# An experts' loop in a pinned order, its output product from two exact parts, and three overflow blocks inside it

## The chip, the core and the metric

The kernel runs on one core of a Trainium2 chip. The metric is the device time of one execution in microseconds (us). Instructions are issued to five engines: PE (matrix products), DVE and ACT (elementwise work), POOL (GpSimd: elementwise work and indirect DMAs) and SP (which only starts DMAs here).

## What is computed

A trunk of two layers over 1024 tokens of width 1024, in f32. Each layer has a modulated norm, one projection that feeds differential attention and an RWKV-7 state scan, an output projection, and then a mixture of 32 experts, of which each token uses two. The part that matters:

```python
def routed_experts(ht, gate_w, expert_id, w_gate, w_up, w_down):
    # each token goes to 2 of 32 experts; rows are sorted by expert, in blocks of ROW_BLOCK = 128
    # per block of one expert:
    #   h = silu(x @ w_gate) * (x @ w_up)      x: 128 x 1024,  h: 128 x 256
    #   y = (h @ w_down) * gate weight         y: 128 x 1024
    ...
```

The reference's sum over the two experts of a token is added to the residual.

## The kernel before

Each layer ends with the experts' loop, `moe` (L1583). It is written for 32 experts with 128 slots each. Tokens of an expert beyond 128 go to overflow blocks, which are run behind the loop, as many as the routing asks for: with these inputs three a layer, so that 35 blocks are computed (70 scatters L1659 in the two layers).

One round of the loop, for expert e:

- `gather` (L1595): POOL fetches 128 rows of the normed input by an indirect DMA into `xg`, two buffers.
- `prepare` (L1603 to L1612): PE transposes them in eight 128x128 pieces (`xT`); ACT makes `xT_hi`, the part that fp32r holds exactly, and DVE the rest, `xT_lo`.
- `split_half` (L1580, L1581): the gate and up weights of an expert come as two halves of 128x2048 (`w_gu`, 1 MB each). Of each, ACT makes `w_hi` and DVE makes `w_lo` = `w_gu` - `w_hi`. There are three pairs of `w_hi` and `w_lo`, so the half that is split during `up(e)` needs the one that `up(e)` has just read.
- `up` (L1628 to L1630): 24 fp32r matmuls of 128x512: `xT_hi` x `w_hi`, `xT_lo` x `w_hi`, `xT_hi` x `w_lo`, in eight slices each.
- `hidden` (L1618 to L1620): ACT's tanh and two DVE instructions give `th`, 128x256.
- `down` (L1649 to L1659), for expert e-1: PE transposes `th` (`hT_ps`), DVE copies it (L1651), PE multiplies it with `w_d` (L1655, `y_ps`) in full f32: four matmuls, eight passes in the trace. DVE scales the result into `yo` (L1658), of which there is one, and POOL scatters its rows to `yd` in DRAM by an indirect DMA (L1659).

The raw weights lie in five `w_gu` and three `w_d` buffers; SP starts their loads four and two experts ahead. An overflow block (L1705 on) computes `up` in full f32 from the raw halves (L1642, 16 passes), under an `If` on the number of blocks.

The order of the instructions on each engine is made by the scheduler of the Tile framework from the order of the code and its dependencies; inside `moe` nothing else sets it.

In the profile's rows, PEld is the weight load of PE, and `w_gu`, `w_hi`, `w_lo`, `w_d`, `xT`, `th`, `yo`, `yd` are the tiles named above. L323, L1210 and L1476 are helpers of earlier stages: splits of other weights on POOL, and one-hot rows of the routing on DVE. L90 is a step of a square root on DVE, L1290 adds a product in PSUM (`po`) to the residual.

Of the kernel before, what the change touches and what calls it, by code (L numbers as in the profile page):

```python
# [10 lines left out]
F32 = mybir.dt.float32  # L11
F32R = mybir.dt.float32r
# [3 lines left out]
OP = mybir.AluOpType  # L16
# [36 lines left out]
class Trunk:  # L53
# [1436 lines left out]
    def route_overflow(self, w, psum):  # L1490
# [20 lines left out]
        big = [w.tile([128, 1024], F32, name="ro_big", tag="ro") for _ in range(2)]  # L1511
        in1, in2 = (x[0:1, 0:480].rearrange("p (b e) -> p b e", e=32) for x in big)
# [9 lines left out]
        tmp = big[0][:, 512:1024].rearrange("p (t e) -> p t e", e=32)  # L1522
# [44 lines left out]
    def load_gu(self, l, i, e):  # L1567

        for half in range(2):
            self.nc.sync.dma_start(self.raw[(2 * i + half) % 5], self.expert_source(l, e, "moe_w_gu")[half])  # L1570

    def load_d(self, l, i, e):
        self.nc.sync.dma_start(self.wd[i % 3], self.expert_source(l, e, "moe_w_down"))

    def split_half(self, n, eng=None):

        nc = self.nc
        raw = self.raw[n % 5]
        lo, hi = self.parts[n % 3]
        nc.scalar.copy(hi, raw)  # L1580
        (eng or nc.vector).tensor_tensor(lo, raw, hi.bitcast(F32), op=OP.subtract)  # L1581

    def moe(self, l, side, psum):  # L1583

        nc, tc = self.nc, self.tc
        with ExitStack() as s:
# [28 lines left out]
            def hidden(ph):  # L1615
                x = tx.tile([128, 512], F32, name="th", tag="mt")
                th = x[:, 0:256]
# [3 lines left out]
                return x  # L1621

            def up(e, x):
                hi, lo = x
                ph = psum.tile([128, 512], F32, name="h_ps", tag="h", bufs=2)
                for k in range(NK):
                    wlo, whi = self.parts[(2 * e + k // 4) % 3]
# [3 lines left out]
                return hidden(ph)  # L1631

            def prepare_late(e):
                pt = transposed(e)
                nc.scalar.copy(late[e % 2], pt)
                return late[e % 2]

            def up_late(e, x):

                ph = psum.tile([128, 512], F32, name="h_ps", tag="h", bufs=2)  # L1640
                for k in range(NK):
                    nc.tensor.matmul(ph, x[:, k, :], self.raw[(2 * e + k // 4) % 5][:, k % 4, :], start=(k == 0), stop=(k == NK - 1))  # L1642
                return hidden(ph)

            def down(e, th):
                w = self.wd[e % 3]
# [10 lines left out]
                yo = tx.tile([128, D], F32, name="yo", tag="x", bufs=1)  # L1657
                nc.vector.scalar_tensor_tensor(yo, po, self.wsl[:, e:e + 1], gt2, op0=OP.mult, op1=OP.mult)  # L1658
                st = nc.gpsimd.indirect_dma_start(out=self.yd, out_offset=bass.IndirectOffsetOnAxis(ap=self.idx_s[:, e:e + 1], axis=0),  # L1659
                                                  in_=yo, in_offset=None, bounds_check=2 * T - 1, oob_is_err=False)  # L1660
                for o in scat:
                    tc.declare_no_dep(st.ins, o.ins, reason="every slot holds another row")
                scat.append(st)
# [4 lines left out]
            def overflow(b):  # L1668
                eb = block_weights(b)
                self.load_gu(l, 32 + b, eb)  # L1670
                self.load_d(l, 32 + b, eb)

            gather(0)
            gather(1)
            x, prev = prepare(0), None
            for e in range(32):
                th = up(e, x)
                for n in (2 * e + 3, 2 * e + 4):
                    if n < 64:
# [20 lines left out]
            gather(33)  # L1700
            self.load_d(l, 32, block_weights(0))
            down(*prev)
            x = prepare_late(32)

            n = nc.values_load(self.ovf[0:1, 0:1], min_val=0, max_val=15)  # L1705
            with ExitStack() as ifs:
                for b in range(15):
                    ifs.enter_context(tc.If(n > b))
                    if b + 2 < 15:
                        gather(34 + b)  # L1710
                    if b + 1 < 15:
                        overflow(b + 1)
                    down(32 + b, up_late(32 + b, x))
                    if b + 1 < 15:
                        x = prepare_late(33 + b)
# [38 lines left out]
    def layer(self, l, x_src):  # L1754

        nc = self.nc
# [12 lines left out]
        def more():  # L1769

            self.wo_stack.close()
            self.more_tiles(se.enter_context(self.pool(name=f"wE{l}", bufs=1, side=here)))
            self.load_gu(l, 1, 1)
            for n in range(3):
                self.split_half(n, nc.gpsimd)
            for e in (2, 3):
                self.load_gu(l, e, e)

        with ExitStack() as s:
            psum = Banks(**{n: s.enter_context(self.pool(name=f"ps{n}e{l}", bufs=b, space=PSUM))  # L1780
                            for n, b in (("tp", 2), ("po", 4), ("pl", 2))})
            self.out_proj(l, there, psum, lambda: (self.load_gu(l, 0, 0), self.load_d(l, 0, 0)), more)
        if l == 0:
            self.dump("xm", self.xm)
        with ExitStack() as s:
            psum = s.enter_context(self.pool(name=f"psE{l}", bufs=1, space=PSUM))
            wp = s.enter_context(self.pool(name=f"wD{l}", bufs=1, side=here))
            self.wd += [wp.tile([128, 2, D], F32, name=f"w_d{i}") for i in range(1, 3)]
            for e in (1, 2):
                self.load_d(l, e, e)  # L1790
            self.moe(l, there, psum)
# [114 lines left out]
```

## Time and profile before

| | us |
|---|---|
| median of three runs | 2879.71 (2871.75 to 2885.03) |
| the profiled execution | 2890.55, span 2888.7 |
| experts' stage, layer 0: first `h_ps` to end of last `y_ps` | 1034.2 to 1441.9 |
| experts' stage, layer 1 | 2427.1 to 2831.3 |

Of the span PE is busy for 85%, DVE 64%, ACT 37%, POOL 25%; the granted clock is 0.903 of full speed on average. The costliest lines are those of the experts' loop and of the input projection. The loop is the stretch where the DMA engines are busiest, between 0.85 and 0.99 of the time.

How to read it: a row of a timeline gives start, duration, engine, line, operation, tiles and shape, and in brackets how long the engine sat idle ahead of it and what ended that. The durations of PE's matmuls overlap; their distance is what counts. In the loop the same pattern returns every 11.07 us.

### The profile page before, as it was taken

The page shows a single profiled execution, that of the slowest core. Times are in us where ns is not written, and L with a number is a line of the kernel's source. Part 1 is how long each engine was busy: PE and PEld are TensorE (multiplying, and loading weights), DVE is VectorE, ACT ScalarE, POOL GpSimd, SP SyncE. Part 2 cuts the span into 40 slices and gives each one's busy share as a digit, 9 for nine tenths or more (in the row PEclk, how much of TensorE's full clock was granted, in tenths as well). Part 3 has the DMA queues.
Part 4 walks back from the last instruction along what each step waited for, and adds up shares of the span by engine and source line. Part 5 has one row for each costly group of instructions (what it writes and reads, how often), then busy time and mean ns, then how long its engine had stood idle before and what let it go on. Part 6 is the DMA issues. An engine that isn't in the chain of part 4 may idle for free.

```text
span 2888.7 us, 45371 instructions
## 1 busy us (share of the span) xinstructions
PE 2452.3 (85%) x17281; PEld 1842.3 (64%) x17281; DVE 1845.5 (64%) x3927; ACT 1063.5 (37%) x1908; POOL 721.3 (25%) x569
## 2 busy tenths in 40 slices
PE   5999987998789779999849888889877986999991
PEld 3766666787678656666427666778756775666650
DVE  5358785555684767767264689756467566776745
ACT  3333332343463224444133343334345331444421
POOL 4122232222420511111141222221242032111113
PEclk8989998998899779999969989899889986999996
DMA  8477575452442359899551434453443224998874
GB/s 285 157 233 215 178 239 135 134 147 93 161 127 93 140 190 328 312 329 336 188 203 52 136 122 140 151 155 115 127 158 114 98 100 147 342 350 317 306 261 186
DMA packets 264230, 548.99 MB, mean 190 GB/s; under 512 B 77048, under 2 KB 181440, under 8 KB 233280
## 3 DMA queue, kind: packets, MB, share of 16 engines
q1 hardware_dynamic: 235424, 490.90, 50.6%
q0 software_dynamic: 23952, 40.99, 3.9%
q10 hardware_dynamic: 4624, 14.06, 1.2%
q8 instruction: 141, 2.31, 0.3%
q14 instruction: 89, 0.73, 0.1%
HBM read 467.68 MB, written 120.09 MB: 203 GB/s over the span
## 4 chain that ended last, share of the span: by engine, by line
PE 52%; DVE 23%; DMA 11%; ACT 7%; issue 5%; POOL 1%; SPq 1%; DVEq 0%; ACTq 0%; POOLq 0%
PE y_ps L1655 8%; PE pj L335 5%; PE pj L336 5%; PE pj L337 5%; DVE w_lo L1581 4%; ACT w_hi L1580 4%; PE h_ps L1629 3%; PE h_ps L1628 2%; DVE sv_m L724 2%; DVE sv_t L726 2%; PE h_ps L1630 2%; PE po L1284 2%; DMA ada_w<-in_ada_w 2%; DMA yd<-yo,idx_s 2%; PE po L1285 2%
## 5 line engine op out<-in xcount | busy, mean ns | idle before, releaser
L1581 DVE TENSOR_TENSOR w_lo<-w_gu,w_hi 128x2048 fp32r<-128x2048 f32 x122 | 279.6, 2292 | 206.3 <-ACT w_hi L1580 202.1
L1580 ACT CAST w_hi<-w_gu 128x2048 fp32r<-128x2048 f32 x128 | 244.0, 1908 | 384.6 <-PE h_ps L1629 367.4
L335 PE MATMUL pj<-hh,wa_hi 128*128 128x512 f32 x800 | 341.6, 427 | 2.7 <-ACT wa_hi L322 1.9
L336 PE MATMUL pj<-hl,wa_hi 128*128 128x512 f32 x800 | 332.0, 415 | 1.1 <-DVE hl L312 1.1
L337 PE MATMUL pj<-hh,wa_lo 128*128 128x512 f32 x800 | 328.9, 413 | 3.3 <-POOL wa_lo L323 3.3
L1655 PE MATMUL y_ps<-w_d,th 128*128 128x512 f32 x560 | 260.3, 608 | 40.9 <-DVE th L1651 25.5
L1628 PE MATMUL h_ps<-w_hi,xT_hi 128*128 128x512 f32 x512 | 225.8, 441 | 3.9 <-ACT xT_hi L1611 3.9
L1629 PE MATMUL h_ps<-w_hi,xT_lo 128*128 128x512 f32 x512 | 210.8, 412 | 2.6 <-DVE xT_lo L1612 2.6
L1630 PE MATMUL h_ps<-w_lo,xT_hi 128*128 128x512 f32 x512 | 203.2, 397 | 0.0
L1655 PEld LDWEIGHTS y_ps<-w_d,th 128*128 128x128 f32 x560 | 101.3, 190 | 156.9 <-issue 103.3
L323 POOL TENSOR_TENSOR wa_lo<-wa_raw,wa_hi 128x1024 fp32r<-128x1024 f32 x50 | 122.0, 2441 | 315.6 <-ACT wa_hi L322 262.0
L335 PEld LDWEIGHTS pj<-hh,wa_hi 128*128 128x128 f32 x800 | 157.8, 197 | 42.0 <-issue 7.4
L337 PEld LDWEIGHTS pj<-hh,wa_lo 128*128 128x128 f32 x800 | 156.8, 196 | 39.5 <-POOL wa_lo L323 4.6
L336 PEld LDWEIGHTS pj<-hl,wa_hi 128*128 128x128 f32 x800 | 157.8, 197 | 37.2 <-issue 4.5
L1659 POOL DMA_INDIRECT yd<-yo,idx_s x70 | 70.5, 1008 | 402.2 <-DVE yo L1658 323.6
L1595 POOL DMA_INDIRECT xg<-h2d,idx_g x74 | 80.1, 1082 | 299.2 <-PE hT_ps L1649 250.7
L1629 PEld LDWEIGHTS h_ps<-w_hi,xT_lo 128*128 128x128 f32 x512 | 98.2, 192 | 50.5 <-DVE xT_lo L1612 30.9
L1658 DVE SCALAR_TENSOR_TENSOR yo<-y_ps,wsl,gt 128x1024 f32<-128x1024 f32 x70 | 89.5, 1279 | 52.2 <-PE y_ps L1655 27.0
L1628 PEld LDWEIGHTS h_ps<-w_hi,xT_hi 128*128 128x128 f32 x512 | 98.4, 192 | 36.7 <-issue 12.9
L724 DVE TENSOR_TENSOR sv_m<-sv_t,sv_n 64x31 f32<-64x31 f32 (+15 forms) x248 | 104.5, 421 | 23.0 <-DMA sv_n<-sp_z 18.5
L1154 ACT ACTIVATE at_p<-at_s,at_mx 128x256 f32<-128x256 f32 (+7 forms) x128 | 94.9, 742 | 63.7 <-DVE at_mx L1152 63.2
L1152 DVE TENSOR_REDUCE at_mx<-at_s 128x1 f32<-128x256 f32 (+7 forms) x128 | 95.8, 753 | 31.3 <-PE at_s L1150 30.4
(438 smaller groups left out, 5428.7 us busy)
## 6 DMA issues: line engine op xcount, KB each, us to landing
w_gu<-in_moe_w_gu SPq DMA_DIRECT2D x144, 1024.0 KB
w_d<-in_moe_w_down SPq DMA_DIRECT2D x72, 1024.0 KB
ada_w<-in_ada_w SPq DMA_DIRECT2D x80, 512.0 KB
wa_raw<-in_w_in SPq DMA_DIRECT2D x50, 512.0 KB
sp_z<-z SPq DMA_DIRECT2D x32, 768.0 KB
b_zz<-sp_z SPq DMA_DIRECT2D x32, 512.0 KB
cy<-yd SPq DMA_DIRECT2D x16, 1024.0 KB
qkv<-qst SPq DMA_DIRECT2D x48, 256.0 KB
```

The costliest lines, as they stand in the source:

```text
L323: nc.gpsimd.tensor_tensor(lo, raw, hi.bitcast(F32), op=OP.subtract)
L335: nc.tensor.matmul(ps, hi[:, k, :], self.hh[k][:, sl], start=(k == 0), stop=False)
L336: nc.tensor.matmul(ps, hi[:, k, :], self.hl[k][:, sl], start=False, stop=False)
L337: nc.tensor.matmul(ps, lo[:, k, :], self.hh[k][:, sl], start=False, stop=(k == NK - 1))
L724: eng.tensor_tensor(t3, tt[:, 0:j + 1, j].unsqueeze(2).to_broadcast([64, j + 1, 31 - j]), nt[:, j, j + 1:32].unsqueeze(1).to_broadcast([64 ...
L1152: nc.vector.tensor_reduce(mx, ps[:, 0:n], axis=AX.X, op=OP.max, negate=True)
L1580: nc.scalar.copy(hi, raw)
L1581: (eng or nc.vector).tensor_tensor(lo, raw, hi.bitcast(F32), op=OP.subtract)
L1628: nc.tensor.matmul(ph, hi[:, k, :], whi[:, k % 4, :], start=(k == 0), stop=False)
L1629: nc.tensor.matmul(ph, lo[:, k, :], whi[:, k % 4, :], start=False, stop=False)
L1630: nc.tensor.matmul(ph, hi[:, k, :], wlo[:, k % 4, :], start=False, stop=(k == NK - 1))
L1655: nc.tensor.matmul(po[:, 512 * half:512 * half + 512], hT[:, k, :], w[:, k, 512 * half:512 * half + 512], start=(k == 0), stop=(k == 1))
```

## The change

Four things change, all in `moe` and what it calls.

1. The output product is made like `up`: `split_d` makes `w_dh` (ACT, L1603) and `w_dl` = `w_d` - `w_dh` (POOL, L1605); `turned` makes the two parts of `hT` (ACT L1679, DVE L1680); PE then runs 12 fp32r matmuls (L1703) `hi` x `w_dh`, `lo` x `w_dh`, `hi` x `w_dl` for four f32 ones. There are two `w_dh` and one `w_dl`; `w_gu` falls from five buffers to four, `w_d` from three to two.
2. The loop runs N = 35 rounds: the three overflow blocks are rounds of it, with weights loaded by the expert's number that SP reads from `ovf`. What is left of the late path starts at the fourth block.
3. Gathers are issued three experts ahead (two before).
4. `in_order` ties the instructions of PE, ACT, DVE and POOL inside the loop to the order in which the code is written, which is new too.

```diff
+    @contextmanager
+    def in_order(self, last):
+        engines = [e.engine for e in (self.nc.tensor, self.nc.scalar, self.nc.vector, self.nc.gpsimd)]
+        traced = self.nc.cur_bb.bb.instructions
+        n = len(traced)
+        yield
+        for i in traced[n:]:
+            if i.engine in engines:
+                if i.engine in last:
+                    self.tc.add_manual_dep(i, last[i.engine].name, ...)
+                last[i.engine] = i
...
+    RAW = 4
...
+    def split_d(self, i, part):
+        hi = self.wdh[i % 2]
+        if part == 0:
+            self.nc.scalar.copy(hi, self.wd[i % 2])
+        else:
+            self.nc.gpsimd.tensor_tensor(self.wdl, self.wd[i % 2], hi.bitcast(F32), op=OP.subtract)
...
+            def turned(e):
+                pt = hidden_turned(e)
+                nc.scalar.copy(hT[:, 0], pt)
+                nc.vector.tensor_tensor(hT[:, 1], pt, hT[:, 0].bitcast(F32), op=OP.subtract)
...
+            def down(e):
+                whi, wlo = self.wdh[e % 2], self.wdl
+                po = psum.tile([128, D], F32, name="y_ps", tag="y", bufs=1)
+                hi, lo = hT[:, 0], hT[:, 1]
+                for n, (x, w) in enumerate(((hi, whi), (lo, whi), (hi, wlo))):
+                    for half in range(2):
+                        cs = slice(512 * half, 512 * half + 512)
+                        for k in range(2):
+                            nc.tensor.matmul(po[:, cs], x[:, k, :], w[:, k, cs], start=(n + k == 0), stop=(n + k == 3))
+                scaled(e, po)
...
-            for e in range(32):
-                th = up(e, x)
-                for n in (2 * e + 3, 2 * e + 4):
-                    if n < 64:
-                        self.split_half(n)
-                if e + 1 < 32:
-                    if e + 2 < 32:
-                        gather(e + 2)
-                    x = prepare(e + 1)
...
-                if prev is not None:
-                    down(*prev)
+            for e in range(N):
+                with self.in_order(last):
+                    ph = up(e, x)
+                    if e + 1 < N:
+                        self.split_half(2 * e + 3)
+                    if e:
+                        turned(e - 1)
+                    if e + 1 < N:
+                        x = prepare(e + 1)
+                    if e + 3 < N:
+                        gather(e + 3)
+                    hidden(e, ph)
+                    self.split_d(e, 0)
...
+                with self.in_order(last):
+                    if e:
+                        down(e - 1)
+                    self.split_d(e, 1)
+                    if e:
+                        scatter(e - 1)
+                    if e + 2 < N:
+                        self.split_half(2 * e + 4)
+                for n in (2 * e + 7, 2 * e + 8):
+                    if n < 2 * N:
+                        self.load_gu(l, n, expert(n // 2))
+                if e + 2 < N:
+                    self.load_d(l, e + 2, expert(e + 2))
```

DVE, one round in the middle of the loop of layer 0, in the program before (`th` of L1651 is the copy of `hT`):

```order
L1658 SCALAR_TENSOR_TENSOR yo<-y_ps,wsl,gt_10476 128x1024
L1581 TENSOR_TENSOR w_lo_10322<-w_gu_10329,w_hi_10323 128x2048
L1651 COPY th<-hT_ps 128x256
L1581 TENSOR_TENSOR w_lo_10326<-w_gu_10330,w_hi_10327 128x2048
L1619 SCALAR_TENSOR_TENSOR th<-th,h_ps 128x256
L1612 TENSOR_TENSOR xT_lo<-xT_ps,xT_hi 128x1024
L1620 TENSOR_TENSOR th<-th,h_ps 128x256
```

and in the program after (L1595 is `w_lo`, L1686 `yo`, L1680 the second part of `hT`, L1638 `xT_lo`):

```order
L1686 SCALAR_TENSOR_TENSOR yo<-y_ps,wsl,gt_10475 128x1024
L1595 TENSOR_TENSOR w_lo_10325<-w_gu_10328,w_hi_10324 128x2048
L1595 TENSOR_TENSOR w_lo_10327<-w_gu_10329,w_hi_10326 128x2048
L1680 TENSOR_TENSOR hT<-hT_ps,hT 128x256
L1638 TENSOR_TENSOR xT_lo<-xT_ps,xT_hi 128x1024
L1644 SCALAR_TENSOR_TENSOR th<-th,h_ps 128x256
L1645 TENSOR_TENSOR th<-th,h_ps 128x256
```

The step that makes `hT` has moved from between the two `w_lo` to behind both.

PE, from the end of one `up` to the start of the next, before:

```order
L1629 MATMUL h_ps<-w_hi_10327,xT_lo 128x512
L1630 MATMUL h_ps<-w_lo_10326,xT_hi 128x512
L1603 MATMUL xT_ps<-ident,xg_10478 128x128 x8
L1649 MATMUL hT_ps<-ident,th 128x128 x2
L1655 MATMUL y_ps<-w_d_9797,th 128x512 x4
L1628 MATMUL h_ps<-w_hi_10325,xT_hi 128x512
```

and after:

```order
L1655 MATMUL h_ps<-w_lo_10323,xT_hi 128x512
L1673 MATMUL hT_ps<-ident,th 128x128 x2
L1629 MATMUL xT_ps<-ident,xg_10477 128x128 x8
L1703 MATMUL y_ps<-w_dh_10470,hT 128x512 x8
L1703 MATMUL y_ps<-w_dl,hT 128x512 x4
L1653 MATMUL h_ps<-w_hi_10324,xT_hi 128x512
```

The transposes of `hT` now stand ahead of those of `xT`, and the output product has become 12 matmuls, of which the last four read `w_dl`.

POOL, in the same stretch after; before, only the scatter L1659 and the gather L1595 stood here, in turn:

```order
L1621 DMA xg_10476<-h2d_614,idx_g 128x1024
L1605 TENSOR_TENSOR w_dl<-w_d_10467,w_dh_10470 128x2048
L1689 DMA yd_615<-yo,idx_s 2048x1024
L1621 DMA xg_10477<-h2d_614,idx_g 128x1024
L1605 TENSOR_TENSOR w_dl<-w_d_9797,w_dh_10469 128x2048
```

The split of `w_d` stands ahead of each scatter.

## Rows read from the trace of the kernel before

**Rows 1.** Chain that ended last, a period of the loop: start us, us, what.

```profile
1186.64 0.23 PE h_ps L1628
...
1187.13 1.92 ACT w_hi L1580
...
1189.08 2.13 DVE w_lo L1581
...
1191.29 0.43 DVE th L1651
```

**Rows 2.** Windows, one period: length, busy us of PE, PEld, DVE, ACT, POOL, PEclk, DMA, GB/s.

```profile
1191.77:1202.84 11.07, 10.45 (x43) 7.02 (x43) 7.91 (x7) 5.00 (x5) 2.08 (x3) 1.00 0.85 311
```

**Rows 3.** Timeline of PE, ends of the stage: start us, us, instruction [idle before].

```profile
1034.22 0.79 PE L1628 MATMUL h_ps<-w_hi,xT_hi 128*128 128x512 f32 x1
...
1061.88 0.48 PE L1628 MATMUL h_ps<-w_hi,xT_hi 128*128 128x512 f32 x1
...
1428.78 7.03 PE L1642 MATMUL h_ps<-w_gu,xT 128*128 128x512 f32 x16
...
1438.21 3.70 PE L1655 MATMUL y_ps<-w_d,th 128*128 128x512 f32 x8 [0.52 <-DVE th L1651]
...
2427.10 0.80 PE L1628 MATMUL h_ps<-w_hi,xT_hi 128*128 128x512 f32 x1
...
2827.61 3.70 PE L1655 MATMUL y_ps<-w_d,th 128*128 128x512 f32 x8 [0.52 <-DVE th L1651]
```

**Rows 4.** Timelines of DVE and POOL at two places where both work.

```profile
983.48 13.87 DVE L1476 TENSOR_SCALAR r_ohr<-r_io,r_rk 128x128 f32<-128x128 f32 x6
...
983.25 13.43 POOL L1581 TENSOR_TENSOR w_lo<-w_gu,w_hi 128x2048 fp32r<-128x2048 f32 x3 [8.43 <-ACT w_hi L1580]
...
850.63 0.68 DVE L1290 TENSOR_TENSOR xm<-xm,po 128x512 f32<-128x512 f32 x1
851.23 1.76 DVE L90 TENSOR_TENSOR rs_u_sub<-rs_u_sub,rs_y_sub 128x4 f32<-128x4 f32 x1
...
853.42 0.16 DVE L90 TENSOR_TENSOR rs_u_sub<-rs_u_sub,rs_y_sub 128x4 f32<-128x4 f32 x1
...
850.55 2.42 POOL L1210 TENSOR_TENSOR wo_0at_q<-wo_raw,wo_0at_q 128x1024 fp32r<-128x1024 f32 x1 [16.62 <-ACT wo_0at_q L1209]
```

**Rows 5.** Scatters and the `yo` that waited; last, groups of 1070 to 1380.

```profile
1352.28 1.01 POOL L1659 DMA_INDIRECT yd<-yo,idx_s  x1 [5.09 <-DVE yo L1658]
...
1362.08 1.28 DVE L1658 SCALAR_TENSOR_TENSOR yo<-y_ps,wsl,gt 128x1024 f32<-128x1024 f32 x1 [0.21 <-DMA yd<-yo,idx_s]
...
1385.75 1.01 POOL L1659 DMA_INDIRECT yd<-yo,idx_s  x1 [5.35 <-DVE yo L1658]
...
1395.94 1.28 DVE L1658 SCALAR_TENSOR_TENSOR yo<-y_ps,wsl,gt 128x1024 f32<-128x1024 f32 x1 [5.09 <-DMA yd<-yo,idx_s]
...
L1658 DVE SCALAR_TENSOR_TENSOR yo<-y_ps,wsl,gt 128x1024 f32<-128x1024 f32 x28 | 35.8, 1279 | 0.2 <-DMA yd<-yo,idx_s 0.2
```

**Rows 6.** DMA queues, 1100 to 1380: packets, MB, share of 16 engines.

```profile
q1 hardware_dynamic: 10660, 77.60, 76.9%
q0 software_dynamic: 7349, 12.02, 11.6%
```

**Rows 7.** Line of the `ovf` reads on SP: ns least, median, most.

```profile
L1666 SPq TENSOR_LOAD <-ovf x10: 265/274/651, 1029.6 to 2796.9; - x10
```

**Rows 8.** Timeline of PE behind two waits of some 2 us.

```profile
313.02 1.09 PE L668 MATMUL tp<-ident,bkb 128*128 128x128 f32 x4 [2.03 <-DVE z L661]
...
315.61 0.63 PE L336 MATMUL pj<-hl,wa_hi 128*128 128x512 f32 x1
...
859.39 0.50 PE L1147 MATMUL at_s<-at_k,at_q 128*128 128x512 f32 x1 [1.92 <-ACT at_p L1154]
859.73 0.39 PE L1150 MATMUL at_s<-at_l,at_q 128*128 128x512 f32 x1
```

More of the change, by code (lines that the diff above doesn't have):

```diff
@@ L2 @@
 import math
-from contextlib import ExitStack, nullcontext
+from contextlib import ExitStack, contextmanager, nullcontext
 import numpy as np
@@ L1565, in expert_source, with load_gu, split @@
         return w if isinstance(e, int) else w[0]
-    def load_gu(self, l, i, e):
-        for half in range(2):
-            self.nc.sync.dma_start(self.raw[(2 * i + half) % 5], self.expert_source(l, e, "moe_w_gu")[half])
+    def load_gu(self, l, n, e):
+        self.nc.sync.dma_start(self.raw[n % self.RAW], self.expert_source(l, e, "moe_w_gu")[n % 2])
     def load_d(self, l, i, e):
-        self.nc.sync.dma_start(self.wd[i % 3], self.expert_source(l, e, "moe_w_down"))
-    def split_half(self, n, eng=None):
[L1577 to L1581, printed above, removed]
+        self.nc.sync.dma_start(self.wd[i % 2], self.expert_source(l, e, "moe_w_down"))
+    def split(self, raw, parts, eng):
+        hi, lo = parts
+        self.nc.scalar.copy(hi, raw)
+        eng.tensor_tensor(lo, raw, hi.bitcast(F32), op=OP.subtract)
+    def split_half(self, n, eng=None):
+        self.split(self.raw[n % self.RAW], self.parts[n % 3], eng or self.nc.vector)
+    def split_d(self, i, part):
[4 more added lines that the diff above has]
+            self.nc.gpsimd.tensor_tensor(self.wdl, self.wd[i % 2], hi.bitcast(F32), op=OP.subtract)
     def moe(self, l, side, psum):
@@ L1630, in up @@
                     nc.tensor.matmul(ph, hi[:, k, :], wlo[:, k % 4, :], start=False, stop=(k == NK - 1))
[L1631 removed]
+                return ph
             def prepare_late(e):
                 pt = transposed(e)
[L1635 to L1636 removed]
+                nc.scalar.copy(late, pt)
+                return late
             def up_late(e, x):
@@ L1641, in up_late, with hidden_turned @@
                 for k in range(NK):
[L1642 to L1646, printed above, removed]
+                    nc.tensor.matmul(ph, x[:, k, :], self.raw[(2 * e + k // 4) % self.RAW][:, k % 4, :], start=(k == 0), stop=(k == NK - 1))
+                hidden(e, ph)
+            def hidden_turned(e):
                 pt = psum.tile([128, 2, 128], F32, name="hT_ps", tag="hT", bufs=1)
@@ new lines, in moe, with scaled, scatter @@
+            yos = {}
+            def scaled(e, po):
+                yo = yos[e] = tx.tile([128, D], F32, name="yo", tag="x", bufs=1)
+                nc.vector.scalar_tensor_tensor(yo, po, self.wsl[:, e:e + 1], gt2, op0=OP.mult, op1=OP.mult)
+            def scatter(e):
+                st = nc.gpsimd.indirect_dma_start(out=self.yd, out_offset=bass.IndirectOffsetOnAxis(ap=self.idx_s[:, e:e + 1], axis=0),
+                                                  in_=yos.pop(e), in_offset=None, bounds_check=2 * T - 1, oob_is_err=False)
+                for o in scat:
+                    tc.declare_no_dep(st.ins, o.ins, reason="every slot holds another row")
+                scat.append(st)
@@ L1656, in down @@
                                          start=(k == 0), stop=(k == 1))
[L1657 to L1663, printed above, removed]
+                scaled(e, po)
+                scatter(e)
             def block_weights(b):
@@ L1669, in overflow, with expert @@
                 eb = block_weights(b)
-                self.load_gu(l, 32 + b, eb)
+                for half in range(2):
+                    self.load_gu(l, 64 + 2 * b + half, eb)
                 self.load_d(l, 32 + b, eb)
+            N = 32 + self.MORE_E
+            def expert(e):
+                return e if e < 32 else block_weights(e - 32)
             gather(0)
             gather(1)
-            x, prev = prepare(0), None
-            for e in range(32):
-                th = up(e, x)
-                for n in (2 * e + 3, 2 * e + 4):
-                    if n < 64:
-                        self.split_half(n)
-                if e + 1 < 32:
-                    if e + 2 < 32:
-                        gather(e + 2)
-                    x = prepare(e + 1)
+            x, last = prepare(0), {}
@@ L1700, in moe @@
[L1700 to L1703, printed above, removed]
+            turned(N - 1)
+            down(N - 1)
+            scatter(N - 1)
+            late = self.lay.tile([128, 8, 128], F32, name="xT", tag="sg")
             n = nc.values_load(self.ovf[0:1, 0:1], min_val=0, max_val=15)
             with ExitStack() as ifs:
-                for b in range(15):
+                for b in range(self.MORE_E, 15):
                     ifs.enter_context(tc.If(n > b))
-                    if b + 2 < 15:
-                        gather(34 + b)
+                    if b == self.MORE_E:
+                        gather(32 + b)
+                        overflow(b)
+                    x = prepare_late(32 + b)
@@ L1772, in more @@
             self.more_tiles(se.enter_context(self.pool(name=f"wE{l}", bufs=1, side=here)))
-            self.load_gu(l, 1, 1)
+            for n in range(2, 4):
+                self.load_gu(l, n, n // 2)
             for n in range(3):
                 self.split_half(n, nc.gpsimd)
-            for e in (2, 3):
-                self.load_gu(l, e, e)
+            for n in range(4, 7):
+                self.load_gu(l, n, n // 2)
         with ExitStack() as s:
@@ L1787, in layer @@
             wp = s.enter_context(self.pool(name=f"wD{l}", bufs=1, side=here))
-            self.wd += [wp.tile([128, 2, D], F32, name=f"w_d{i}") for i in range(1, 3)]
-            for e in (1, 2):
-                self.load_d(l, e, e)
+            self.wd += [wp.tile([128, 2, D], F32, name="w_d1")]
+            self.wdl = wp.tile([128, 2, D], F32R, name="w_dl")
+            self.wdh = [wp.tile([128, 2, D], F32R, name=f"w_dh{i}") for i in range(2)]
+            self.load_d(l, 1, 1)
             self.moe(l, there, psum)
```

55 lines of the change are left out of this document (28 added, 27 removed).

## Prediction

> **What bounds the kernel now.** I read the views in this order: the chain of waits, the windows of the experts' loop, the ends of the loop on PE, and then the rows that price what is new.
>
> In the steady part of the loop the chain runs through three engines [rows 1]. When half of an expert's `up` is through (a new matmul every 0.227 us, printed as 0.23), ACT makes `w_hi` (1.92), DVE makes `w_lo` (2.13, and its next instruction starts 2.21 after it), then comes the copy of `hT` that stands behind `w_lo` on DVE (0.43), then PE's output product `y_ps` in full f32 (3.70 [rows 3]), then the next `up`. That repeats every 11.07 us. One period [rows 2] has PE busy for 10.45, DVE 7.91, ACT 5.00, POOL 2.08, at a granted clock of 1.00 and with the DMA engines at 0.85. So PE loses only about 0.6 us of each period: the loop is nearly bound by PE, and f32 passes of the output product are the part of PE's work that can be made smaller.
>
> The whole stage, from the first `h_ps` to the end of the last `y_ps`, takes 1438.21 + 3.70 - 1034.22 = 407.7 us in layer 0 and 2827.61 + 3.70 - 2427.10 = 404.2 in layer 1, three overflow blocks included [rows 3]; both together 811.9. The first two experts need 27.7 of it (1034.22 to 1061.88).
>
> **The change, part by part.** *PE.* Per expert `y_ps` becomes 12 matmuls at 0.227 = 2.72 in place of 3.70, so PE's work falls from 10.45 to 9.47. The three overflow blocks lose their f32 `up` (7.03 [rows 3]) and become three more rounds of the loop, 35 in all. If PE alone counted, 35 rounds at 9.5 would save over 60 us a layer.
>
> *ACT* gains the cast `w_dh` (as `w_hi`, 1.92) and a small copy of `hT`: 5.00 + 2.3 = 7.3, below any period in question; nothing.
>
> *POOL* gains `w_dl` = `w_d` - `w_dh`, 128x2048. POOL has done this operation on this shape: three in 13.43 us, 4.48 each [rows 4]. POOL would then be busy for 2.08 + 4.5 = 6.6, no bound by itself. But it has two costs. First, `w_dl` has one buffer: the split for expert e can start only when the last matmuls of the product of e-1 have read it. Second, what DVE does beside it. In [rows 4] six small DVE instructions (L1476) beside those three POOL splits took 13.87 us. Better still is the place at 850.55, where POOL runs a TENSOR_TENSOR for 2.42: DVE's L1290, which reads one input from PSUM (`po`), passes in 0.68 in the midst of it; DVE's L90, both inputs in SBUF, starts at 851.23 and takes 1.76, to 852.99, POOL's end being 852.97, though the same instruction takes 0.16 at 853.42. So `yo`, `hT`, `xT_lo` (PSUM inputs) can run beside `w_dl`, and `w_lo` (both inputs in SBUF) cannot.
>
> The Trainium skill, page "SBUF — State Buffer", section "Who interferes with whom", says the same of a VectorE instruction with two SBUF inputs: whichever of it and a GpSimd instruction that reads SBUF starts first has the shared ports to its end, and the other is blocked. It speaks against this change. By it the sum is the one below with the lock; had DVE and POOL run side by side, it would be the first rival. No run here shows `w_lo` itself beside `w_dl`.
>
> *DVE.* Its new order behind `down(e-1)` is `yo`, `w_lo`, `w_lo`, `hT`, `xT_lo`, `th`, `th`. `yo` waits for the end of `down(e-1)`, the very moment that releases POOL's `w_dl`. So POOL always starts first, and both `w_lo` stand behind it. And `hT` lo, which the second third of the next output product needs, stands behind both. That closes a loop which does not go through PE's `up` at all:
>
> `w_dl` 4.48 + `w_lo` 2.21 + `w_lo` 2.21 + `hT` lo 0.43 + eight matmuls (`lo`x`w_dh`, `hi`x`w_dl`) 8 x 0.227 = 1.82 + hand-overs and the last matmul's way out 0.3 (each hand-over in [rows 1] is 0.02 to 0.08) = **11.45 us**, longer than today's 11.07. PE waits 2.0 of it (11.45 - 9.47), ahead of `lo`x`w_dh`.
>
> *Scatter and `yo`.* `yo` keeps its single buffer, so it waits for the scatter before it. The scatter now stands behind `w_dl` on POOL, 4.5 later than today. From issue to free buffer it took 9.8 in the loop (1352.28 to 1362.08) and 10.2 (1385.75 to 1395.94) at the loop's end [rows 5]; those are waits that showed, most are shorter. `yo` may be late until `w_dl` ends, without any loss: 11.45 - 4.5 from the next `down`, plus 4.5 - 1.28. That is, up to 10.2 from the issue. I take 0, at the edge.
>
> *DMA.* q1 and q0 take 76.9 + 11.6% [rows 6] of 11.07, that is 9.8 us an expert. Fewer raw buffers (4 for 5, 2 for 3) leave less slack, but each load still has over 14 us between its buffer's release and its use at 11.45. Nothing, while the period stays over 9.8. Ten reads of `ovf` (three before) now stand on SP ahead of the loop's loads: 7 x 0.27 = 2 us [rows 7], covered by the 27.7 of the start; up to +2 a layer if not.
>
> *Clock.* PE's 0.6 us of waiting becomes one wait of 2.0. The trace has both answers to such a wait: behind 2.03 us of idle time at 313.02 a 128x512 matmul shows 0.63 (315.61), behind 1.92 at 859.39 it shows 0.39 (859.73) [rows 8]. 0.63 is the lower of the two clock levels, and some 0.2 more for each. If the slow stretch meets the eight matmuls of the loop, it costs 8 x 0.2 = 1.6 a round; if it meets `up`, nothing, as `up` has the 2.0 to spare, and it then shortens the next wait. Bounds 0 and 1.6. I take 0.2: half of the waits, and about a quarter of the price in those. The period is then **11.65**.
>
> *Sum.* A layer is 27.7 (first two rounds, as before) + 32 periods + the last round's end. That end was 1441.91 - 1428.78 = 13.1 [rows 3]; it loses 1.6 of `up`, 1.0 of `xT` transposes (ten transposes have 10.45 - 5.45 - 3.70 = 1.3 of a period, eight of them 1.0), 1.0 of `y_ps` and gains 0.4 for the second `hT`: 10. So 27.7 + 32 x 11.65 + 10 = 410.5, against 407.7 and 404.2: +2.8 and +6.3, **+9 us**. With no clock loss at all (11.45) it is 404.1: -4. Everything before and behind the loop is unchanged.
>
> The profiled execution took 2890.55 (span 2888.7), 10.8 above the median of 2879.7; the difference goes to the median: 2879.7 + 9 = **2889**. Periods of 11.3 to 12.0 give -13 to +32: 2867 to 2912.
>
> **The rivals.** *No lock for `w_lo`* (or POOL's split placed so that it costs nothing). Then the period is the largest of PE 9.5, DMA 9.8 and the scatter's own loop, latency + `yo` 1.28 + 0.1: 11.0 at 9.6, below 9.8 at 8.4. 10.4 is the middle: 2 x (27.7 + 332.8 + 10) - 811.9 = -71, **2809**; ends 9.8 (2770) and 11.0 (2847). For it: L90 and L1476 are small instructions beside `w_lo`, which [rows 4] don't show at such a place. Against it: both waited to POOL's end.
>
> *The scatter decides* (slower). If it takes more than 10.2 us behind a `w_dl`, the period is latency + 1.4: at 11.0, 12.4. Then 27.7 + 396.8 + 10 = 434.5 a layer, +57: **2937**. For it: 10.2 was seen. Against it: with 9.7 between a scatter and the next `yo` (11.07 - 1.28 - 0.1), 28 `yo` of the loop waited 0.2 for it in all [rows 5].
>
> *The clock falls in every round* (slower): 13.05 a period, 2 x 455.3 - 811.9 = +99, **2979**. For it: 2.03 at 313.02; against it: 1.92 at 859.39, and a slow `up` closes the wait that caused it.
>
> *The change doesn't do what it says*: a fourth overflow block, or a late path that is still entered, would add rounds. 35 scatters a layer before mean three blocks, and the loop now runs 35 rounds; I give it nothing of its own.
>
> **How the numbers follow.** The lock's case 0.60, no lock 0.24, the scatter 0.10, the clock 0.06. Within the lock's case, a change of more than 0.5% (14 us, about what a measurement of this kernel can tell from no change) is +14 in 3 of 10 (periods over 11.73), -14 in 1 of 20. So slower 0.16 + 0.18 = 0.34, faster 0.24 + 0.03 = 0.27, within 0.39. The range leaves out the fast half of the no-lock case and the clock's: 2809 to 2945, some 0.8.
>
> **What would show it.** Right: POOL L1605 at 4.5; DVE L1595 right behind `yo` with 4 to 5 us on its row instead of 2.29, ended with POOL's; PE with 2 us of wait ahead of L1703, released by DVE `hT` L1680; periods of 11.4 to 11.9. Wrong: L1595 at 2.29 while POOL runs, PE waits under 1 us, periods of 10 to 10.5. For the scatter: `yo` L1686 ending later than `w_dl`, released by the DMA of `yd`. For the clock: a granted clock below 0.9 in the loop and matmuls of 0.63.

## The result: 3.1% slower

The changed kernel takes 2969.05 us (2966.14 to 2971.32), the kernel before 2881.15: a ratio of 1.031, with an interval of 1.0289 to 1.0331. The forecast was 2889, the range 2809 to 2945. So the change costs 88 us where +9 was expected, and the time lies above the range.

The ends of the stage on PE, of the changed kernel, answer to [rows 3]:

```profile
1018.47 0.78 PE L1653 MATMUL h_ps<-w_hi,xT_hi 128*128 128x512 f32 x1
...
1474.06 1.20 PE L1703 MATMUL y_ps<-w_dl,hT 128*128 128x512 f32 x4 [1.28 <-POOL w_dl L1605]
...
2453.02 0.77 PE L1653 MATMUL h_ps<-w_hi,xT_hi 128*128 128x512 f32 x1
...
2901.66 1.20 PE L1703 MATMUL y_ps<-w_dl,hT 128*128 128x512 f32 x4 [1.31 <-POOL w_dl L1605]
```

The stage takes 456.8 and 449.8 us, 906.6 in place of 811.9: +94.7, more than the whole loss. The rest is 19 less in these two executions (2057.6 against 2076.8). I count no gain from that: before's profiled execution was 9 above its median, and in variants of the changed kernel whose edits all lie inside the loop the rest is 2059.4 (e1 below), 2070.0 (e11) and 2080.8 (e12).

A window of 310 us in the loop, first of the kernel before:

```profile
1110.00:1420.00 310.00, 289.54 (x1134) 189.89 (x1133) 202.33 (x184) 125.69 (x103) 56.98 (x55) 0.99 0.86 311
```

Then the same window of the changed kernel (columns as in [rows 2]) and the lines of POOL's split, `w_lo` and the scatter (ns least, median, most; the last two are what `yo` waited for, us and times, and the time from a scatter's issue to its landing, which frees `yo`):

```profile
1110.00:1420.00 310.00, 258.21 (x1108) 205.59 (x1107) 200.58 (x169) 172.23 (x144) 223.01 (x72) 0.90 0.77 281
...
L1605 POOL TENSOR_TENSOR w_dl<-w_d,w_dh x70: 4540/4612/4702, 1030.8 to 2897.1; 128x2048 fp32r<-128x2048 f32 x70
...
L1595 DVE TENSOR_TENSOR w_lo<-w_gu,w_hi x134: 2275/2283/5772, 1025.9 to 2882.9; 128x2048 fp32r<-128x2048 f32 x134
...
L1689 POOL DMA_INDIRECT yd<-yo,idx_s x70: 970/2810/3009, 1048.9 to 2908.6; - x70
...
  DMA yd<-yo,idx_s: 251.6, 57
...
DMA to landing us min/median/max: 2.6/10.8/12.5
```

No engine is near full: PE 0.83 of the window, POOL 0.72, DVE 0.65. The granted clock is 0.90, before 0.99. And two rows say what wasn't in the sum: the scatter's instruction takes 2.81 us in place of 1.01 [rows 5], and `yo` waits for a scatter in 57 of 70 rounds. 23 rounds of layer 0, from the scatter at 1142.29 to the one at 1438.70, take 12.89 each; from the 5th to the 29th `yo` of both layers the mean is 12.86, where 11.65 was forecast.

One slow round of the changed kernel, timelines of POOL, DVE and PE:

```profile
1204.98 2.88 POOL L1689 DMA_INDIRECT yd<-yo,idx_s  x1 [0.17 <-issue]
...
1211.91 4.61 POOL L1605 TENSOR_TENSOR w_dl<-w_d,w_dh 128x2048 fp32r<-128x2048 f32 x1 [1.85 <-ACT w_hi L1594]
...
1204.14 5.04 DVE L1595 TENSOR_TENSOR w_lo<-w_gu,w_hi 128x2048 fp32r<-128x2048 f32 x2
1209.10 0.41 DVE L1680 TENSOR_TENSOR hT<-hT_ps,hT 128x256 fp32r<-128x256 f32 x1
...
1216.23 1.28 DVE L1686 SCALAR_TENSOR_TENSOR yo<-y_ps,wsl,gt 128x1024 f32<-128x1024 f32 x1 [4.81 <-DMA yd<-yo,idx_s]
1217.43 4.48 DVE L1595 TENSOR_TENSOR w_lo<-w_gu,w_hi 128x2048 fp32r<-128x2048 f32 x2
1221.83 0.42 DVE L1680 TENSOR_TENSOR hT<-hT_ps,hT 128x256 fp32r<-128x256 f32 x1
...
1222.30 2.08 PE L1703 MATMUL y_ps<-w_dh,hT 128*128 128x512 f32 x4 [3.17 <-DVE hT L1680]
1224.18 1.91 PE L1703 MATMUL y_ps<-w_dl,hT 128*128 128x512 f32 x4
```

Read it from the scatter. It is issued at 1204.98, just after a `w_lo` has begun (the two `w_lo` of the row at 1204.14 wait for POOL's split, which ends at 1204.82, and end at about 1206.9 and at 1209.18). 1204.98 + 2.88 is 1207.86, some 0.9 behind the end of the first `w_lo`: about the scatter's own time, once it may start. `yo` gets its buffer at 1216.23, 11.25 after the issue. The split that began at 1211.91 ends at 1216.52, while `yo` still runs, so it is `yo` that holds up the two `w_lo` behind it, these hold up `hT`, and PE waits 3.17. The eight matmuls then run at the lower clock, 3.8 in place of 2.1 us.

### The profile page after: what moved, and what is told of

It reads as the page before. It is cut to its first block, busy times and chain, and to the rows that moved or that the text cites. A ratio compares the mean times of both kernels' runs of the same rounds, so it can differ in the third digit from the quotient of the medians.

```text
span 2964.3 us, 46373 instructions
## 1 busy us (share of the span) xinstructions
PE 2439.1 (82%) x17593; PEld 1938.8 (65%) x17593; DVE 1929.7 (65%) x3945; ACT 1234.9 (42%) x2058; POOL 1208.3 (41%) x635
## 3 DMA queue, kind: packets, MB, share of 16 engines
q8 instruction: 144, 2.36, 0.3%
## 4 chain that ended last, share of the span: by engine, by line
PE 21%; DVE 13%; DMA 8%; issue 4%; ACT 2%; SPq 1%; POOL 1%; another core or an unknown queue 0%; DVEq 0%; POOLq 0%; ACTq 0%
DMA yd<-yo,idx_s 4%; DVE w_lo L1595 4%; PE pj L350 2%; PE pj L352 2%; PE y_ps L1703 2%; PE pj L351 2%; DMA sp_z<-z 1%; DVE sv_m L739 1%; PE at_o L1196 1%; PE po L1299 1%; PE po L1300 1%; PE po L1301 1%; DVE xm L1795 1%; PE rb_y L899 1%; DVE sv_t L741 1%
## 5 line engine op out<-in xcount | busy, mean ns | idle before, releaser
L1605 POOL TENSOR_TENSOR w_dl<-w_d,w_dh 128x2048 fp32r<-128x2048 f32 x70 | 322.9, 4613 | 200.2 <-PE y_ps L1703 166.0
L1594 ACT CAST w_hi<-w_gu 128x2048 fp32r<-128x2048 f32 x140 | 267.8, 1914 | 266.0 <-PE h_ps L1654 265.9
L1595 DVE TENSOR_TENSOR w_lo<-w_gu,w_hi 128x2048 fp32r<-128x2048 f32 x134 | 344.9, 2611 | 14.9 <-ACT w_hi L1594 14.9
L1703 PE MATMUL y_ps<-w_dh,hT 128*128 128x512 f32 x560 | 186.1, 461 | 131.0 <-DVE hT L1680 126.8
L1686 DVE SCALAR_TENSOR_TENSOR yo<-y_ps,wsl,gt 128x1024 f32<-128x1024 f32 x70 | 89.9, 1284 | 281.9 <-DMA yd<-yo,idx_s 251.6
L1655 PE MATMUL h_ps<-w_lo,xT_hi 128*128 128x512 f32 x560 | 226.4, 404 | 0.0
L1703 PEld LDWEIGHTS y_ps<-w_dh,hT 128*128 128x128 f32 x560 | 104.9, 208 | 174.3 <-DVE hT L1680 153.5
L1689 POOL DMA_INDIRECT yd<-yo,idx_s x70 | 186.5, 2665 | 48.8 <-DVE yo L1686 30.8
L1621 POOL DMA_INDIRECT xg<-h2d,idx_g x70 | 126.8, 1811 | 63.7 <-PE ro_pv L1564 22.2
L922 POOL TENSOR_TENSOR b_y<-b_y,b_lnx 128x512 f32<-128x512 f32 x16 | 20.9, 1306 | 282.0 <-issue 179.3
L1603 ACT CAST w_dh<-w_d 128x2048 fp32r<-128x2048 f32 x70 | 133.1, 1902 | 0.0
```

What stands on the lines that cost most here:

```text
L1594: self.nc.scalar.copy(hi, raw)
L1595: eng.tensor_tensor(lo, raw, hi.bitcast(F32), op=OP.subtract)
L1603: self.nc.scalar.copy(hi, self.wd[i % 2])
L1605: self.nc.gpsimd.tensor_tensor(self.wdl, self.wd[i % 2], hi.bitcast(F32), op=OP.subtract)
L1703: nc.tensor.matmul(po[:, cs], x[:, k, :], w[:, k, cs], start=(n + k == 0), stop=(n + k == 3))
```

## The experiments

All times are medians; the kernel before took 2877 to 2883 on the same chips. A round is the mean distance from the 5th to the 29th `yo`, both layers of the profiled execution; the kernel before has 11.08.

| kernel | us | ratio to before | round, us |
|---|---|---|---|
| changed | 2969.1 | 1.031 (1.029 to 1.033) | 12.86 |
| e1: second `yo` | 2945.2 | 1.023 (1.021 to 1.025) | 12.44 |
| e12: PE's wait filled | 2955.5 | 1.026 (1.023 to 1.029) | 12.40 |
| e11: both | 2914.1 | 1.013 (1.009 to 1.017) | 11.75 |
| e2: `w_dl` on DVE | 2891.2 | 1.003 (1.001 to 1.006) | 11.61 |
| e8: e2 and second `yo` | 2814.7 | 0.978 (0.976 to 0.979) | 10.46 |
| e3: no `w_dl` | 2853.9 | 0.990 (0.989 to 0.992) | 11.19 |
| e7b: product of before | 2885.6 | 1.002 (1.000 to 1.004) | 11.68 |
| e5: order not pinned | 3037.2 | 1.054 (1.049 to 1.059) | 13.52 |
| e6: overflow behind the loop | 3025.8 | 1.050 (1.046 to 1.054) | 12.74 |
| e9: before, DVE work with two SBUF inputs | 2901.4 | 1.006 (1.004 to 1.009) | 11.08 |
| e10: before, DVE work with a PSUM input | 2889.4 | 1.003 (1.001 to 1.005) | 11.07 |

Two theories stood at the start. *S*: the scatter decides, because POOL's DMA instruction is held up by `w_lo`. *C*: POOL's split, the lock and the lower clock decide, and `yo`'s wait only fills idle time.

**A second `yo` buffer (e1).**

```diff
-                lo = xp.tile([128, 8, 128], F32R, name="xT_lo", tag="xT_lo")
+                lo = xp.tile([128, 8, 128], F32R, name="xT_lo", tag="xT_lo", bufs=1)
...
-                yo = yos[e] = tx.tile([128, D], F32, name="yo", tag="x", bufs=1)
+                yo = yos[e] = self.yo2 if e % 2 else tx.tile([128, D], F32, name="yo", tag="x", bufs=1)
```

> The changed kernel with a second yo buffer (4 KB taken from a second xT_lo buffer that PE's order leaves unused). In the changed kernel a round takes 12.87 us and yo L1686 waits for the scatter before it in 57 of 70 rounds. Theory S (the scatter decides: POOL's DMA instruction starts behind w_dl, while DVE runs w_lo, and shows 2.8 us instead of 1.0; scatter to free yo 11.2, + 1.28 + 0.3 = 12.8): the wait is gone, the round falls to that of the loop w_dl, w_lo, w_lo, hT, eight matmuls, 11.6 to 12.0 with some slow matmuls; about 66 rounds x 1.0 = 66 less, 2890 to 2915 us. Rival C (the lock and the lower clock decide, yo's wait only fills DVE's idle time): yo no longer waits, but the round stays at 12.7 to 12.9, 2955 to 2970 us.

2945.2, between the two. `yo` no longer waits for a DMA, yet a round still takes 12.4. The window of e1, and two rounds of it on POOL, DVE and PE:

```profile
1110.00:1420.00 310.00, 265.04 (x1146) 211.43 (x1145) 281.37 (x173) 175.63 (x148) 232.13 (x74) 0.91 0.76 290
...
1212.67 4.62 POOL L1605 TENSOR_TENSOR w_dl<-w_d,w_dh 128x2048 fp32r<-128x2048 f32 x1 [1.88 <-PE y_ps L1703]
1225.95 4.63 POOL L1605 TENSOR_TENSOR w_dl<-w_d,w_dh 128x2048 fp32r<-128x2048 f32 x1 [3.42 <-PE y_ps L1703]
...
1213.66 7.97 DVE L1595 TENSOR_TENSOR w_lo<-w_gu,w_hi 128x2048 fp32r<-128x2048 f32 x2
1221.56 0.41 DVE L1680 TENSOR_TENSOR hT<-hT_ps,hT 128x256 fp32r<-128x256 f32 x1
...
1222.03 1.99 PE L1703 MATMUL y_ps<-w_dh,hT 128*128 128x512 f32 x4 [2.13 <-DVE hT L1680]
1223.82 1.89 PE L1703 MATMUL y_ps<-w_dl,hT 128*128 128x512 f32 x4
```

The two `w_lo`, 4.5 us of work, stand there for 7.97, as the first waits for the split to end at 1217.29: the lock of the prediction. The matmuls behind `hT` lo start 9.36 us after the start of the split in all the 12 rounds between 1200 and 1350; what varies is what comes behind them: 11.7 where the eight matmuls run at the higher clock, up to 13.3 where, as here, they take 1.8 + 1.9.

**PE's wait filled (e11, e12).** To tell the clock from the wait, PE's wait is taken away: the four matmuls `hi` x `w_dh` are run three times there, and the last time counts.

```diff
-                for n, (x, w) in enumerate(((hi, whi), (lo, whi), (hi, wlo))):
+                for n, (x, w) in enumerate(((hi, whi), (hi, whi), (hi, whi), (lo, whi), (hi, wlo))):
...
-                            nc.tensor.matmul(po[:, cs], x[:, k, :], w[:, k, cs], start=(n + k == 0), stop=(n + k == 3))
+                            nc.tensor.matmul(po[:, cs], x[:, k, :], w[:, k, cs], start=(n < 3 and k == 0), stop=(k == 1 and n in (0, 1, 4)))
```

> e1_yo2 with PE's wait filled: the four matmuls hi x w_dh are run three times (each time from a fresh start, the last one counts), 1.8 us more of PE work in the place where PE waits 2.1 us for hT lo. In e1_yo2 every round has hT lo 9.36 us after the start of w_dl, and the eight matmuls behind it then take 2.1 us in some rounds and up to 3.9 in others; rounds 11.7 to 13.3, mean 12.5. Theory K (the wait makes the granted clock fall, and the fall costs 0.8 a round): granted clock near 1.00 in the loop, rounds 11.7, 66 x 0.8 = 53 less than e1_yo2's 2945, 2880 to 2905 us. Rival (the slow matmuls have another cause, or the eight matmuls too many are in the way): no gain, 2940 to 2965 us.

> The changed kernel with PE's wait filled as in e11_yo2_fill (hi x w_dh three times), and one yo buffer. In e11_yo2_fill, with two yo buffers, every round was 11.72 at a granted clock of 1.00; in e1_yo2, without the filling, 12.5; the changed kernel has 12.87. With the clock kept up and yo still waiting for the scatter, theory S (scatter to free yo 10.8 in the mean, yo 1.28, 0.3 to 0.8 to the next scatter) has rounds of 12.1 to 12.5, 2930 to 2950 us. If yo's wait is only a consequence of the slow rounds, it goes too: rounds of 11.7, 2905 to 2920 us.

e11 has eight matmuls more a round than e1 and is 31 us faster. Its window, and two rounds of PE:

```profile
1110.00:1420.00 310.00, 301.45 (x1423) 243.55 (x1424) 301.02 (x189) 188.90 (x158) 245.33 (x79) 1.00 0.81 308
...
1215.97 1.20 PE L1703 MATMUL y_ps<-w_dh,hT 128*128 128x512 f32 x4 [0.30 <-DVE hT L1680]
1217.01 1.08 PE L1703 MATMUL y_ps<-w_dl,hT 128*128 128x512 f32 x4
...
1227.68 1.19 PE L1703 MATMUL y_ps<-w_dh,hT 128*128 128x512 f32 x4 [0.29 <-DVE hT L1680]
1228.72 1.08 PE L1703 MATMUL y_ps<-w_dl,hT 128*128 128x512 f32 x4
```

The granted clock is 1.00 and nearly every round is 11.7: this is the loop through the lock as the prediction drew it, by itself. The total of 2914 is 9 above the expected range: its two stages are 44.7 shorter than e1's (837.7 against 882.4), 0.7 a round, and what lies outside them took 11 longer in e11's profiled execution, though nothing was changed there. In e12, with one `yo` buffer, the clock is 1.00 as well:

```profile
1110.00:1420.00 310.00, 286.62 (x1355) 231.24 (x1354) 201.68 (x179) 180.90 (x151) 231.95 (x76) 1.00 0.79 291
```

But its rounds between 1200 and 1350 take 11.7 to 13.0, as the scatter lets them: in the 62 rounds in which `yo` waited, it got its buffer 10.4 us after the issue in the mean. 2955.5 is 6 above what S expected. So the clock costs 0.7 a round where `yo` is free (12.44 to 11.75) and 0.46 where it isn't (12.86 to 12.40); the scatter costs 0.42 on top of the slow clock and 0.65 without it. Each covers part of the other.

**What holds the scatter up (e9, e10).** To the kernel before, two DVE instructions of 1.22 us are added behind each `yo`, in DVE's idle time.

```diff
                 nc.vector.scalar_tensor_tensor(yo, po, self.wsl[:, e:e + 1], gt2, op0=OP.mult, op1=OP.mult)
+                for _ in range(2):
+                    nc.vector.tensor_tensor(dump, yo, gt2, op=OP.mult)
```

e10 has `po`, the tile `y_ps`, in place of `yo` in the last line. In both, `dump` takes the room of the second `xT_lo` buffer.

> The kernel before with two more DVE instructions behind each yo: yo x gt2 into a tile that nobody reads, 128x1024, 1.22 us each, both inputs in SBUF. They lie in the 3.07 us in which DVE waits for w_hi, so nothing of DVE's work is late by them. The scatter L1660 starts 0.3 us behind yo, 0.9 before the first of them ends. If POOL's DMA instruction can't start beside a DVE instruction with two SBUF inputs: it shows 1.8 to 2.0 us instead of 1.01, yo waits for the scatter in some rounds, 2880 to 2915 us. If it can: 1.01, 2875 to 2890 us.

> The counterpart: the two instructions behind yo multiply y_ps with gt2, one input in PSUM, the same shape and time. If it is the second SBUF input that holds POOL's DMA instruction up, the scatter shows 1.01 as in the kernel before, 2875 to 2890 us; if it is any DVE work beside it, 1.8 to 2.0 us.

The scatter's line and its time to landing, first in e9, then in e10:

```profile
L1662 POOL DMA_INDIRECT yd<-yo,idx_s x70: 1732/1867/2054, 1055.6 to 2840.9; - x70
...
DMA to landing us min/median/max: 3.4/6.7/10.7
```

```profile
L1662 POOL DMA_INDIRECT yd<-yo,idx_s x70: 970/1012/1024, 1058.9 to 2841.5; - x70
...
DMA to landing us min/median/max: 2.6/7.9/9.7
```

One operand is another, and the scatter's instruction takes 1.87 or 1.01, at the same round of 11.1. And its end lies 0.84 to 0.91 behind the end of the DVE instruction beside which it started, in all 70 rounds of e9 and in all 64 of the changed kernel where that was a `w_lo`. So a POOL DMA that finds a DVE instruction with two SBUF inputs under way waits for its end. The Trainium skill, page "SBUF — State Buffer", section "Who interferes with whom", infers that a `tensor_tensor` leaves descriptor generation alone, because it takes only the read side of the shared ports; for this indirect DMA, which reads its indices from SBUF, the measurement says otherwise. Here the 0.9 us cost hardly anything, as `yo` seldom waits in that loop (4 times in e9): the two stages take 815.0 us in e9 and 817.5 in e10, so the 12 us between the two lie elsewhere.

**`w_dl` on DVE (e2), and with a second `yo` (e8).**

```diff
-            self.nc.gpsimd.tensor_tensor(self.wdl, self.wd[i % 2], hi.bitcast(F32), op=OP.subtract)
+            self.nc.vector.tensor_tensor(self.wdl, self.wd[i % 2], hi.bitcast(F32), op=OP.subtract)
```

> The changed kernel with w_dl made on DVE instead of POOL, between yo and the two w_lo; one yo buffer. POOL then runs indirect DMAs alone, and w_lo can't wait for it. Theory S: the scatter still starts while DVE runs an instruction with two SBUF inputs (w_dl now), so L1689 still shows 2.5 to 3 us, scatter to free yo 10.8 to 11, round 12.3 to 12.6, 2930 to 2950 us. Rival C (POOL's w_dl, the lock and the clock decide): the loop through DVE is yo 1.28, w_dl 2.2, w_lo 2.2, w_lo 2.2, hT 0.43, eight matmuls 1.8, 0.4 = 10.5, 2805 to 2830 us.

> Both edits: w_dl on DVE and a second yo buffer. Theory S and rival C: no wait for POOL's split and none for the scatter, round 10.5 (DVE's 8.2 + 2.2 of work and the way through the matmuls), 2805 to 2830 us. Under S the step from one yo buffer to two is worth 110 to 130 us here, under C nothing.

e2: the scatter's line, and what `yo` waited for:

```profile
L1689 POOL DMA_INDIRECT yd<-yo,idx_s x70: 972/2799/3001, 1048.0 to 2826.3; - x70
...
  DMA yd<-yo,idx_s: 58.8, 36
```

With no split on POOL the scatter still takes 2.80: it now meets `w_dl` on DVE. Theory S had that right and its price wrong: `yo` waits in 36 rounds, not in all, and 2891 is 39 below S's range and 61 above C's. The shortest rounds are the 10.4 of the loop through DVE. The second `yo` buffer is worth 76 us here, and e8 is **faster than both kernels, 2814.7**. A round of it on DVE and POOL:

```profile
1203.31 1.28 DVE L1686 SCALAR_TENSOR_TENSOR yo<-y_ps,wsl,gt 128x1024 f32<-128x1024 f32 x1 [0.29 <-PE y_ps L1703]
1204.51 2.28 DVE L1605 TENSOR_TENSOR w_dl<-w_d,w_dh 128x2048 fp32r<-128x2048 f32 x1
1206.71 4.49 DVE L1595 TENSOR_TENSOR w_lo<-w_gu,w_hi 128x2048 fp32r<-128x2048 f32 x2
1211.12 0.42 DVE L1680 TENSOR_TENSOR hT<-hT_ps,hT 128x256 fp32r<-128x256 f32 x1
...
1213.77 1.28 DVE L1686 SCALAR_TENSOR_TENSOR yo<-y_ps,wsl,gt 128x1024 f32<-128x1024 f32 x1 [0.31 <-PE y_ps L1703]
...
1204.88 2.80 POOL L1689 DMA_INDIRECT yd<-yo,idx_s  x1 [3.21 <-DVE yo L1686]
```

DVE does 2.2 us more than in the changed kernel and never waits for POOL; 10.46 from one `yo` to the next.

**No `w_dl` at all (e3).** The split and the four matmuls `hi` x `w_dl` are left out.

> The changed kernel without w_dl: POOL's split and the four matmuls hi x w_dl are left out, so the output product lacks that part. One yo buffer. Theory S: yo is followed at once by w_lo on DVE, the scatter starts beside it and shows 2.5 to 3 us, round 12.2 to 12.6 although PE has only 8.6 us of work and POOL no split: 2925 to 2950 us. Rival C: round 9.8 (DMA) to 10.4, 2765 to 2805 us.

2853.9, far above what C forecast and far under what S did. The scatter's line, what `yo` waited for, and `w_lo`:

```profile
L1689 POOL DMA_INDIRECT yd<-yo,idx_s x70: 967/2798/2816, 1046.5 to 2797.1; - x70
...
  DMA yd<-yo,idx_s: 189.9, 59
...
L1595 DVE TENSOR_TENSOR w_lo<-w_gu,w_hi x134: 2278/2284/2294, 1030.7 to 2775.2; 128x2048 fp32r<-128x2048 f32 x134
```

`yo` waits in 59 rounds, though PE has only 8.6 us of work a round. It got its buffer 9.5 us after the issue in the mean of these, in e12 10.4: the time behind the instruction varies from kernel to kernel, and S had taken it as fixed. What makes it vary is not shown. And no `w_lo` is longer than 2.29: POOL's DMA waits for DVE, but DVE didn't wait for the DMA.

**The rest of the change alone (e7b).** The product of before (three `w_d` buffers, `hT` copied whole) in the pinned loop with the early gathers and the overflow rounds. A first form of it, e7 (2898.1), loaded `w_d` of e+2 over that of e ahead of its use, so it computes something else; nothing rests on it.

> The changed kernel with the output product of before (hT copied whole by DVE, four f32 matmuls from w_d, three w_d buffers again, no w_dh and no w_dl): the pinned order, the early gathers and the overflow blocks in the loop alone. PE's work is 10.45 a round; the way from the end of one product to that of the next is yo 1.28, w_lo 2.2, w_lo 2.2, hT 0.43, y_ps 3.70, 0.4 = 10.2. Theory S: the scatter still starts beside w_lo, shows 2.8 us, and yo waits for it in part of the rounds: 11.0 to 11.5, 2850 to 2880 us. Without that wait: rounds of 10.5 to 10.7, 2815 to 2835 us.

2885.6, no difference from before, and 6 above what S expected. `yo` waits in 41 rounds, 138 us in all, behind a scatter of 2.80. That the scatter beside `w_lo` takes what the pinned loop could have gained on its own fits this; e7b with a second `yo` buffer, which would show it, was not run.

**The order (e5) and the overflow blocks (e6).**

```diff
-                if i.engine in last:
+                if False:
                     self.tc.add_manual_dep(...)
```

```diff
-    MORE_E = 3
+    MORE_E = 0
```

> The changed kernel without the pinned order: the scheduler orders the same instructions. DVE's row still has yo, w_lo, w_lo ahead of hT, and POOL's has w_dl ahead of the scatter. If the order's pinning is the cause of the loss: 2880 to 2900 us. If the cause is w_dl on POOL and its place, whoever orders it: 2950 to 2990 us.

> The changed kernel with the three overflow blocks behind the loop again, in full f32, as in the kernel before (the loop has 32 rounds). In the kernel before a late block took 12.97 us and the way from the loop into them 13.6 more; in the changed kernel a round takes 12.87, the last ones 9 to 10. If moving them is a gain of its own: 2980 to 3010 us. If it is nothing: 2960 to 2975 us.

Both are gains of the change, 68 and 57 us: 3037 and 3026 lie above all that was expected. A wait of PE in e5, and two at the end of the loop in e6:

```profile
1207.41 1.20 PE L1703 MATMUL y_ps<-w_dh,hT 128*128 128x512 f32 x4 [1.21 <-ACT hT L1679]
```

```profile
1433.08 3.75 PE L1703 MATMUL y_ps<-w_dh,hT 128*128 128x512 f32 x8 [7.09 <-DVE yo L1686]
...
1444.96 1.97 PE L1629 MATMUL xT_ps<-ident,xg 128*128 128x128 f32 x8 [6.89 <-DMA xg<-h2d,idx_g]
```

Without the pinned order ACT makes `hT` behind both `w_hi`, PE waits 1.2 for it in 60 rounds, and rounds are 13.5. In e6 the loop's last product waits 7.09 for `yo`, and from its end at 1438.1 to the first block's `up` at 1448.03 PE has the block's transposes to do (1.97) and waits 8.0, 6.89 of it for the block's gather. In the loop both waits lie beside other experts' work.

## Why the prediction was wrong

*The lock: right, and 0.3 short.* `w_lo` waits for POOL's split, `hT` stands behind it, and the loop through them is longer than 11.07. Forecast 11.45; measured by itself in e11 it takes 11.72 in nearly every round, 11.75 in the mean. The split takes 4.61 instead of 4.48, and from the start of the eight matmuls to the next split 2.36 go by (11.72 less 9.36), where the sum had 1.82 and part of 0.3.

*The clock: right mechanism, under a third of its size.* The term was 0.2 of a possible 1.6. It is 0.7 (e1 against e11). The step that failed is "half of the waits, and about a quarter of the price": in the 12 rounds of e1 between 1200 and 1350, 8 have slow matmuls behind the wait, and these are 12.85 long in the mean, the other four 11.71. The slow stretch begins soon after the wait ends, where the eight matmuls are (1.99 for the first four at 1222.03, 1.20 in e11), not somewhere in the round.

*The scatter: the step that failed most plainly.* "I take 0, at the edge", with 10.2 as the limit. It is 0.42 on top of the slow clock (the changed kernel against e1), 0.65 without it. It was priced with the scatter's instruction at 1.0, as it was where DVE had nothing to do beside it. The order rows showed two `w_lo` behind `yo` on DVE, and the same lock that was read from [rows 4] for POOL's TENSOR_TENSOR was not applied to POOL's DMAs. The way from the issue to the landing is 10.8 in the median, past the limit; in e10, whose rounds are those of before, it is 7.9. Of the 2.9 between them the longer instruction on POOL is 1.8; the rest stays open, and so does why it is only 6.7 in e9, where the instruction is longer too. A row of before could have raised the question: the gather L1595 had a median of 1067 ns and a longest of 1998.

Together 0.3 + 0.5 + 0.4 = 1.2 a round, over 64 rounds 77 of the 80 us between forecast and result. These are steps from run to run (11.45, 11.75, 12.44, 12.86), so they must add up; in another order the clock would have less of it and the scatter more. The rivals were priced alone (2937 for the scatter, 2979 for the clock) and each given a small chance, but they came together, and neither needed the other: e1 has the slow matmuls without the scatter's wait, e12 the wait without the slow matmuls. The range ended just above the price of the scatter alone.

*Right:* PE's work fell, and neither ACT (0.56 of the window) nor the DMA engines (0.77) bound the loop, which no longer goes through `up`. The overflow blocks were counted as three more rounds, and that held; behind the loop they would have cost 57 us more (e6). *Not priced:* the pinned order by itself, without which it would have been 68 us worse (e5). The earlier gathers and the fewer raw buffers were not varied by themselves.

## What to carry to other kernels

When work is added to POOL or moved beside it, check each POOL instruction, indirect DMAs too, against the DVE instructions that will stand beside it. Here a DVE instruction with two SBUF inputs waited for POOL's elementwise split to its end, and POOL's DMAs waited for such a DVE instruction. A single buffer behind a DMA of 8 to 11 us is a loop of its own (latency + its writer), and a small lengthening of either end makes it the bound. Where a change puts a wait of 2 us ahead of PE's critical matmuls, count them at the lower clock in a good part of the rounds (here 8 of 12).

## What the runs showed of the hardware

An indirect DMA on POOL waits for a DVE instruction with two SBUF inputs that is under way (1.87 and 2.80 against 1.01). It is through some 0.9 us behind the end of that one, also where the next such instruction follows directly, and it didn't delay that next one (no `w_lo` of e3 is longer than 2.29). Useless matmuls can pay: eight more a round, run in PE's wait, kept the granted clock at 1.00 instead of 0.91 and made the kernel 31 us faster.
